# Column slices of 256, 424 and 424 in place of 336, 384 and 384, and one feature tile pair for all columns

## The chip, the cores and the metric

The kernel runs on one core of one Trainium2 chip. The metric is the device time of one execution in microseconds (us). The profile is one execution taken by the hardware profiler; its engines are called PE (TensorE), PEld (TensorE's weight loads), DVE (VectorE), ACT (ScalarE), POOL (GpSimd) and SP (SyncE, which here only issues transfers).

## The reference, cut to what matters

One inference step of a two-layer decoder: an mLSTM layer and a forgetting-attention (FoX) layer, each with an output projection added to the hidden state and a SwiGLU FFN behind it. There are 1104 token columns: 64 sample tokens and 16 meta tokens (together 80), then 1024 prompt tokens. The width D is 1024, the FFN's 2816, all float32.

```python
xn = rmsnorm(x, g)
p  = xn @ w_in                        # q, k, v, output gate, gates i and f
h, state = mlstm_sequence(q, k, v, li, lf, state0, lead)
x  = x + (rmsnorm(h, mh_g) * sigmoid(og)) @ w_out
a, b = split(rmsnorm(x, g_f) @ w_gate_up)
x  = x + (silu(a) * b) @ w_down       # FFN, once in each layer
...
x  = x + (o * sigmoid(og)) @ w_out    # second layer; o: attention with per-row log-forget values
...
x  = x + (silu(a) * b) @ w_down
y  = rmsnorm(x, g_final)
```

## The kernel before, in words

**Layout.** Activations lie feature-major: 128 features on the partitions, 8 such blocks (KT) for D, and tokens as columns. The columns are cut into three slices TS; each is made of three token tiles (the first tile has 80 tokens, the others 128): 336, 384 and 384 columns, SL = 384. A matmul loads a 128x128 block of weights and moves one slice of columns through it.

**Precision.** Every float32 operand is split into a high and a low fp32r part (L243 on ACT, L244 on DVE), and a product is three matmuls: high by high, high by low, low by high (L170 to L172).

**The features of the current layer step** stand in `X[t]`, a pair of tiles (high, low) for each slice, allocated anew by `new_x` whenever the features are written again, which orders the new writer behind the readers of the old tile. Reading a token tile goes through `x_tile`.

**Layer 0.** `phase_a` loads and norms the tokens, projects them, and runs the mLSTM over chunks. The values of all heads stand in three tiles `vA`. `gate_head` (L1247) transposes a head's result (PE L1256), multiplies it with the output gate read back from HBM by POOL (DVE L1257, in tiles ogqk, ogeb, ogc), and splits it into the features.

**The output projection** (`mlp`, L395) has a `unit(t, m)` for each slice t and output block m: 24 matmuls, an addition into the hidden state (DVE L462) and its squares for the norm. In layer 0 the units of slice 0 run between the gating of the later heads, and the weights of m = 0 to 2 (`wo`) come split from HBM by six SP loads (L440), that of m = 3 (`woraw`) is loaded raw and split, and m = 4 to 7 come raw through two slots and are split there (L447). In layer 1 all eight come raw through two slots. Stores of the mLSTM's end state (`out_p_C`, `out_p_n`, L967 and L968) are also issued by SP; out_p_n is written in elements of four bytes.

**The FFN** (`ffn`, L1263) computes slice 0 plainly and slices 1 and 2 together by Winograd's form of Strassen's product: seven products in place of eight, of halves of the weights, slices and features. The up projection has 22 `Unit`s a layer: 48 plain matmuls of slice 0 (two column blocks of w_gate and w_up, 24 each, tile fps) and 84 product matmuls (L1314). The down projection (L1633, tile dps) has 528 plain and 924 product matmuls a layer. The operands of the products are sums and differences of slices, made by DVE; at the FFN's start `TwoNorms` (L90 to L151) norms slice 2 and makes these for the first time, while PE runs the plain blocks of the first Units. Results of the up projection go to HBM (hT, hB) and come back through POOL's queue (`hr`, L1454).

**The end of layer 0's FFN** feeds `first_values` (L1725), which reads token tiles of the normalized features; `final` (L1674) norms, transposes (tile fin) and stores the output of a slice in three token tiles, two halves of the width each (DVE L1715), with the sums of squares from PE (tile fss, L1698).

**What sets the order.** PE's order is the program's, by hand, in the projections and the FFN; in the FFN's start and loop DVE's and ACT's are as well. The queues of SP and POOL, and DVE and ACT in layer 0's output projection, are ordered by a list scheduler, so that a change of sizes can move instructions there.

Of the kernel before, what the change touches and what calls it, by code (L numbers as in the profile page):

```python
# [16 lines left out]
P = 128  # L17
D = 1024
KT = D // P
# [10 lines left out]
TS = [(TT[g[0]][0], TT[g[-1]][1]) for g in GRP]  # L30
SL = max(b - a for a, b in TS)
# [14 lines left out]
class PairWeights:  # L46

    def __init__(self, net, w, slots, H):  # L50
        self.net, self.w = net, w
        cut = lambda t, a=0: t[:, a : a + KT * P].rearrange("p (k n) -> p k n", k=KT)
        flat = [h.rearrange("p k n -> p (k n)") for h in H]
        self.raw = [(cut(slots[0]), cut(slots[1])), (cut(flat[0]), cut(flat[0], KT * P)),
                    (cut(flat[2], 4 * SL), cut(flat[1], 2 * KT * P))]
        self.both = [(cut(slots[2 + i]), cut(slots[6 + i])) for i in range(4)]
# [33 lines left out]
class TwoNorms:  # L90
# [63 lines left out]
class Net:  # L154
# [109 lines left out]
    def new_x(self, t):  # L264

        n = TS[t][1] - TS[t][0]
        self.X[t] = tuple(
            self.xp.tile([P, KT, n], F32R, name=self.uid(f"x{t}{s}"), tag=f"x{t}{s}") for s in "hl"
        )
        return self.X[t]  # L270

    def x_tile(self, i, k):

        t = i // 3
        o = TS[t][0]
        a, b = TT[i][0] - o, TT[i][1] - o
        xh, xl = self.X[t]
        return xh[:, k, a:b], xl[:, k, a:b]
# [44 lines left out]
    def norm_x(self, H, t, g, sp, pp, inplace=False, psum=False):  # L323
# [8 lines left out]
        for i in GRP[t]:  # L332
            yield
            rs = r[:, TT[i][0] - t0 : TT[i][1] - t0]
            nc.vector.reciprocal(rs, rs)
        xh, xl = self.new_x(t)
# [38 lines left out]
    def run(self):  # L375
        nc, tc, I, O, ctx = self.nc, self.tc, self.I, self.O, self.ctx
        self.consts()
        self.hD = self.dram.tile([P, KT, T], F32, name="hD")
        self.X = {}
        self.wmin = 0  # L380
        self.slots = None
        cy, cb = ExitStack(), ExitStack()
        with ExitStack() as c1:
            self.xp = c1.enter_context(self.pool("x"))
            with ExitStack() as c2:

                vp = c2.enter_context(self.pool("vH"))
                vt = [vp.tile([P, 3 * HA * (DV + 1)], F32, name=f"vA{t}") for t in range(3)]
                heads = self.phase_a(vt)
                H = [v[:, : KT * (t1 - t0)].rearrange("p (k n) -> p k n", k=KT) for v, (t0, t1) in zip(vt, TS)]  # L390
# [162 lines left out]
def load_x(self):  # L553

    nc, I = self.nc, self.I
    with self.pool("lx", bufs=2) as lp, self.pool("lxp", bufs=2, space=PSUM) as pp:
        gr = lp.tile([P, D], F32, name="gr", bufs=1)
        nc.scalar.dma_start(gr, I["norm_a"][0].partition_broadcast(P))
        for i, (t0, t1) in enumerate(TT):
            n = t1 - t0  # L560
            if i % 3 == 0:
                self.new_x(i // 3)
# [14 lines left out]
            for g in range(2):  # L577
# [5 lines left out]
                o = t0 - TS[i // 3][0]  # L583
                xh, xl = self.X[i // 3]
                self.split(ps[:, :, :n], xh[:, ks, o : o + n], xl[:, ks, o : o + n])
# [9 lines left out]
def phase_a(self, vt):  # L595
# [4 lines left out]
    v = lambda i: vt[i // 3][:, i % 3 * HA * (DV + 1) : (i % 3 + 1) * HA * (DV + 1)].rearrange(  # L600
        "p (h d) -> p h d", h=HA)
    with ExitStack() as c3:
# [88 lines left out]
        def heads(pp, tag, op=None, some=None):  # L691
# [4 lines left out]
            def ahead():  # L696
                if todo:
                    t, h = todo.pop(0)
                    og = op(self.uid("ogc")) if callable(op) else op.pop(0)
                    nc.gpsimd.dma_start(og[:, : TS[t][1] - TS[t][0]], ogD[h, :, TS[t][0] : TS[t][1]])  # L700
                    ready.append(og)
# [174 lines left out]
def recurrence(self, kp, rec, v, qkD, fill, gate):  # L876
# [12 lines left out]
    with ExitStack() as cr, self.pool("recAp", bufs=2, space=PSUM) as pp:  # L889
# [28 lines left out]
        with self.pool("rec2") as sets[2], self.pool("rec1", bufs=2) as rp, self.pool("rec3") as sets[0]:  # L918
# [8 lines left out]
            for i in range(1, NT):  # L927
# [16 lines left out]
                if i in (6, 7):  # L944

                    for x in ("qk", "eb"):
                        y = sets[i % 3].tile([P, 1024], F32, name=f"og{x}{i}", tag=x,
                                             bufs=2 if x == "eb" and i == 7 else None)
                        places += [y[:, z : z + SL] for z in (0, 512)]
# [297 lines left out]
def gate_head(self, t, h, v, og, pp, tag):  # L1247

    nc = self.nc
    yh, yl = self.X[t] if h else self.new_x(t)  # L1250
    g0, g1 = TS[t]
# [7 lines left out]
    self.split(og[:, :n], yh[:, h, :], yl[:, h, :])  # L1259
# [3 lines left out]
def ffn(self, H, l, weights, order, norm, each, after, end, early=None):  # L1263
# [16 lines left out]
    with self.pool(f"ffn{l}") as fp, self.pool(f"ffnp{l}", space=PSUM) as pp:  # L1280
# [4 lines left out]
        fs += [flat[0][:, 2048 : 2048 + SL]] + [flat[2][:, a : a + SL] for a in (0, SL, 2 * SL, 3 * SL, 2560)]  # L1285
# [170 lines left out]
        def h_split(y):  # L1456
            if y < len(hseq):
# [3 lines left out]
                else:  # L1461
                    o = [y for t, n in ((0, 3), (1, 4), (2, 4)) for y in cut(self.X[t], n)][c]
                r = hraw.pop(y)
                m, n = r.shape[1:]
                hpart[t, z if t else 0, c] = tuple(p[:, : m * n].rearrange("p (k n) -> p k n", k=m) for p in o)
# [208 lines left out]
def final(self, H, t, gr, sp, pools):  # L1674
# [3 lines left out]
    s0 = TS[t][0]  # L1678
    r = sp.tile([P, 3], F32, name=self.uid("fr"), tag="fr", bufs=2)
# [4 lines left out]
    out = [out[:, x % 5 * 512 : x % 5 * 512 + 512] for x in range(6)]  # L1684

    def turn(i, t0, t1):
# [8 lines left out]
    def root():  # L1695
        ss = pn.tile([P, 512], F32, name=self.uid("fss"), tag="n")
        for y, (_, a, b) in enumerate(tiles):
# [9 lines left out]
    for x, (i, t0, t1) in enumerate(tiles):  # L1707
        L = t1 - t0
        ps = turn(i, t0, t1)
        if t == 2 and x == 0:  # L1710
            root()
        for g in range(2):
# [4 lines left out]
            if i == 0:  # L1717
                nc.sync.dma_start(O["y_sample"].rearrange("b t d -> (b t) d")[:, gs], o[:NS])
            else:
                nc.sync.dma_start(O["y_prompt"][0, (i - 1) * P : i * P, gs], o)  # L1720
# [4 lines left out]
def first_values(self, fp, pp, norm):  # L1725
# [4 lines left out]
    for t in range(3):  # L1730
        vs = self.ny(f"vf{t}").rearrange("p k t -> p (k t)").rearrange("p (i d) -> p i d", i=3)
# [59 lines left out]
def phase_b(self, ys, w7, cb):  # L1791
# [11 lines left out]
    with self.pool("fb", bufs=2) as fp, self.pool("fbp", bufs=2, space=PSUM) as pp:  # L1803
# [38 lines left out]
        for w, g, gi, dst, dstS in ((wkv, G_KV, 0, self.kD, self.kS), (wqo, G_B, 1, self.qD, self.qS)):  # L1842
            gcol = gc[:, gi : gi + 1]
            for c in range(4):
# [12 lines left out]
                def turn(q, v4, c=c, raw=raw, gi=gi, gcol=gcol, dst=dst, dstS=dstS):  # L1857
                    for hp in range(2):
                        f = 2 * c + hp
                        ps = pp.tile([P, 512], F32, name=self.uid("btp"), tag="bt")  # L1860
                        g0, g1 = TS[q]
# [5 lines left out]
                        hi = fp.tile([P, SL], F32R, name=self.uid("bhi"), tag="bhi")  # L1867
                        lo = fp.tile([P, SL], F32R, name=self.uid("blo"), tag="blo")
# [71 lines left out]
def forget(self, lf):  # L1940

    nc, I, O = self.nc, self.I, self.O
    with self.pool("fg") as fp, self.pool("fgp", bufs=1, space=PSUM) as pp:
# [9 lines left out]
        for q in range(3):  # L1953
            ps = pp.tile([HB, 512], F32, name=f"fgps{q}", tag="fg")
            g0, g1 = TS[q]
# [311 lines left out]
def attend_prompt(self, ys):  # L2267
# [3 lines left out]
    with self.pool("ap", bufs=1) as sp, self.pool("ap2", bufs=2) as s2, self.pool("app", bufs=2, space=PSUM) as pp:  # L2271
# [159 lines left out]
        def units(hp, g):  # L2431
# [8 lines left out]
            for j0 in range(0, nf, 2):  # L2440
# [32 lines left out]
                def prod(j0=j0, tail=tail, hold=hold):  # L2473
# [54 lines left out]
        with tc.manual_schedule(engines={E.PE, E.DVE, E.Activation, E.Pool}):  # L2528
# [22 lines left out]
            for hp, g in groups:  # L2551
                us = None
                for k in range(g + 1):
                    n = len(todo_exp)
                    ahead(slot)
                    if slot == 0:
                        for _ in gate:
                            pass
                        for t in range(3):
                            self.new_x(t)  # L2560
# [53 lines left out]
```

## Time and profile before

| | |
|---|---|
| time, median of 3 runs | 2905.01 us (2904.12 to 2905.68) |
| span of the profiled execution | 2904.6 us |
| PE busy | 97% |
| DVE, ACT, POOL busy | 58%, 40%, 28% |
| mean granted PE clock | 0.991 |
| HBM traffic | 159 GB/s over the span |

A row of a group or of the timeline gives the line of the kernel, the engine, the tile written and those read, their shapes and the time; in the chain of waits each row is the start, the length and the piece of work that led to the end. "x84" is a count of instructions. In a table of stretches the columns are the stretch, its length, the busy time of PE, PEld, DVE, ACT and POOL (with the number of instructions), the granted PE clock, the share of the DMA engines, and GB/s. Matmul durations overlap, since matmuls are pipelined; some of their records are missing.

### The profile page before, as it was taken

To read this page: it belongs to the slowest core of one execution; us is meant where nothing else is said; L and a number is where in the kernel's file an instruction comes from. 1 tells how busy PE (TensorE), PEld (TensorE's weight loads), DVE (VectorE), ACT (ScalarE), POOL (GpSimd) and SP (SyncE) were. 2 spreads that over 40 slices of the span, in tenths; PEclk is the share of its full clock that TensorE was granted. 3 is DMA by queue.
4 is the path that set the end of the run, shared out by engine and by line. 5 is a ranking of instruction groups with operands and counts; after the bars stand their busy time and mean duration, and the time that the engine had idled before them with its cause. 6 is when DMAs were issued, how large, how long until landed. Compare 5 with 4: busy or idle time off the path is not lost.

```text
span 2904.6 us, 53405 instructions
## 1 busy us (share of the span) xinstructions
PE 2819.4 (97%) x20709; PEld 2702.2 (93%) x20709; DVE 1687.8 (58%) x3292; ACT 1151.6 (40%) x2103; POOL 827.6 (28%) x1225
## 2 busy tenths in 40 slices
PE   7999989999999999999999899999999999999998
PEld 7999879999999999999999787677899999999998
DVE  5032565876776555672445443777477677655565
ACT  5222463422222244453444444877332222224343
POOL 2021232332232221134352101454323223222122
PEclk9999999999999999999999999999999999999999
DMA  7153555244444375664454775443324444437574
GB/s 249 49 142 96 138 172 148 89 148 148 148 150 152 107 259 198 225 210 130 137 169 130 235 280 201 131 163 105 121 95 149 147 148 151 152 106 237 185 248 145
DMA packets 381625, 464.43 MB, mean 160 GB/s; under 512 B 37571, under 2 KB 302747, under 8 KB 380347
## 3 DMA queue, kind: packets, MB, share of 16 engines
q1 hardware_dynamic: 341058, 323.68, 35.1%
q0 software_dynamic: 37904, 135.88, 14.5%
q8 instruction: 163, 2.67, 0.4%
q10 hardware_dynamic: 2408, 1.46, 0.2%
q14 instruction: 92, 0.75, 0.1%
HBM read 324.63 MB, written 136.29 MB: 159 GB/s over the span
## 4 chain that ended last, share of the span: by engine, by line
PE 78%; DVE 6%; ACT 2%; issue 2%; DMA 2%; POOL 0%; DVEq 0%; SPq 0%; ACTq 0%; POOLq 0%
PE m L1314 21%; PE dps L1633 16%; PE fps L172 4%; PE fps L171 4%; PE fps L170 4%; PE tmps L170 3%; PE tmps L171 3%; PE tmps L172 3%; PE sp L2401 2%; PE pops L172 1%; PE pops L170 1%; PE pops L171 1%; PE op L2488 1%; DVE s L2405 1%; PE mmA L170 1%
## 5 line engine op out<-in xcount | busy, mean ns | idle before, releaser
L244 DVE TENSOR_TENSOR slot<-slot,slot 128x1024 fp32r<-128x1024 f32 (+1 forms) x152 | 194.8, 1283 | 141.5 <-ACT slot L243 141.1
L243 ACT CAST slot<-slot 128x1024 fp32r<-128x1024 f32 (+1 forms) x152 | 152.9, 1007 | 200.1 <-PE dps L1633 98.7
L172 PE MATMUL fps<-x0h,slot 128*128 128x336 f32 x688 | 218.2, 317 | 1.6 <-DVE slot L244 1.6
L170 PE MATMUL fps<-x0h,slot 128*128 128x336 f32 x688 | 218.0, 317 | 0.0
L171 PE MATMUL fps<-x0l,slot 128*128 128x336 f32 x688 | 217.4, 316 | 0.0
L1314 PE MATMUL m<-x2h,slot 128*128 128x384 f32 x704 | 193.7, 336 | 0.0
L1314 PE MATMUL m<-x1h,slot 128*128 128x384 f32 x672 | 185.0, 336 | 0.0
L172 PEld LDWEIGHTS fps<-x0h,slot 128*128 128x128 f32 x688 | 129.1, 188 | 2.1 <-DVE slot L244 2.1
L170 PEld LDWEIGHTS fps<-x0h,slot 128*128 128x128 f32 x688 | 129.3, 188 | 0.6 <-ACT slot L243 0.5
L171 PEld LDWEIGHTS fps<-x0l,slot 128*128 128x128 f32 x688 | 129.5, 188 | 0.1
L1314 PEld LDWEIGHTS m<-x2h,slot 128*128 128x128 f32 x704 | 128.5, 188 | 0.0
L1314 PEld LDWEIGHTS m<-x1h,slot 128*128 128x128 f32 x672 | 122.5, 188 | 0.1
L1633 PE MATMUL dps<-T_1h,slot 128*128 128x384 f32 x448 | 118.9, 340 | 0.0
L1314 PE MATMUL m<-x2l,slot 128*128 128x384 f32 x352 | 118.4, 336 | 0.0
L1633 PE MATMUL dps<-T_2h,slot 128*128 128x384 f32 x448 | 117.6, 338 | 0.0
L244 DVE TENSOR_TENSOR slot<-Ht,slot 128x1024 fp32r<-128x1024 f32 x59 | 83.7, 1418 | 54.5 <-ACT slot L243 54.5
L244 DVE TENSOR_TENSOR slot<-vA,slot 128x1024 fp32r<-128x1024 f32 x59 | 83.7, 1418 | 54.5 <-ACT slot L243 54.5
L1314 PE MATMUL m<-x1l,slot 128*128 128x384 f32 x336 | 112.8, 336 | 0.0
L321 POOL TENSOR_TENSOR ns<-ns,nq 128x384 f32<-128x384 f32 (+1 forms) x62 | 75.5, 1218 | 106.0 <-ACT nq L319 104.1
L1314 PE MATMUL m<-T_2h,slot 128*128 128x384 f32 x352 | 97.8, 338 | 2.0 <-DVE slot L244 2.0
L2428 ACT ACTIVATE s<-s,nb 128x272 f32<-128x272 f32 (+7 forms) x126 | 98.9, 787 | 0.0
L1314 PE MATMUL m<-T_4h,slot 128*128 128x384 f32 x352 | 97.8, 338 | 0.6 <-DVE vA L1295 0.6
(783 smaller groups left out, 9157.1 us busy)
## 6 DMA issues: line engine op xcount, KB each, us to landing
slot<-in_w_down SPq DMA_DIRECT2D x48, 512.0 KB, 4.6
slot<-in_w_gate_up SPq DMA_DIRECT2D x36, 512.0 KB, 4.2
ws<-in_w_down SPq DMA_DIRECT2D x88, 192.0 KB, 2.9
sD<-ws SPq DMA_DIRECT2D x88, 192.0 KB, 2.1
kp<-in_cache_k SPq DMA_DIRECT2D x32, 512.0 KB, 6.1
vp<-in_cache_v SPq DMA_DIRECT2D x32, 512.0 KB, 5.5
hr<-hB_T POOLq DMA_DIRECT2D x40, 384.0 KB, 5.1
vA<-in_w_gate_up SPq DMA_DIRECT2D x26, 512.0 KB, 3.9
```

The source lines that it names most:

```text
L170: mm(ps, sh, mh, start=first, stop=False)
L171: mm(ps, sh, ml, start=False, stop=False)
L172: mm(ps, sl, mh, start=False, stop=last)
L243: self.nc.scalar.copy(hi, src)
L244: self.nc.vector.tensor_tensor(out=lo, in0=src, in1=hi.bitcast(F32), op=ALU.subtract)
L321: (nc.vector if x >= late else nc.gpsimd).tensor_tensor(out=s, in0=s, in1=sq, op=ALU.add)
L1314: nc.tensor.matmul(u.ps[b], w[p][:, k], x[q][:, k], start=first and k == i == 0, stop=k == 3 and i == 2, skip_group_check=True)
L1633: nc.tensor.matmul(o, p[:, k, ms], q[:, k], start=fresh and k == x == 0, stop=last and k == nk - 1 and x == 2, skip_group_check=True)
L2401: nc.tensor.matmul(ps[z][:, :n], a[r, qs], b[r, at : at + n], start=(y == 0), stop=(y == 2))
L2405: nc.vector.tensor_tensor_reduce(out=ss[z, u][:, at + o : at + e], in0=ps[z][:, o:e], in1=diag[x][:, z] if y else ncb[:, z, at + o : at + ...
L2428: nc.scalar.activation(ss[z, u], ss[z, u], AF.Exp, bias=nb[:, z : z + 1], accum_out=sm[:, u, z : z + 1])
L2488: mm(po[ds[z], :256], vr[:, j0 + x, ds[z]], th[:, x, z], start=(j0 + x == 0), stop=False)
```

## The change

The slices become 256, 424 and 424 columns. They no longer end where token tiles end; where the program goes by token tiles (gating, the attention's transposes, the forget gates) it takes the old groups, now TG with the width GL. The features are one pair of tiles for all 1104 columns, and `X[t]` are views into it; `new_x` is gone. `vA` is one tile. The reciprocals of a norm go in three equal pieces of a slice. One scratch piece of the FFN comes from another pool, as a block that held it is now too small. `final` cuts the slices into pieces of their own: (80, 88, 88), and four of 106 for each of the other two. In the attention, POOL's copies of 256 columns are no longer split at a slice's border. The scratch for descriptors of POOL's DMAs is set to 8192 bytes in the program's constructor, which had no such setting.

```diff
-TS = [(TT[g[0]][0], TT[g[-1]][1]) for g in GRP]
-SL = max(b - a for a, b in TS)
+TG = [(TT[g[0]][0], TT[g[-1]][1]) for g in GRP]
+GL = max(b - a for a, b in TG)
+SL = 424
+TS = [(0, T - 2 * SL), (T - 2 * SL, T - SL), (T - SL, T)]
+def pieces_of(n, m=3):
+    w = -(-n // m)
+    return [(a, min(a + w, n)) for a in range(0, n, w)]
...
     def inverse(self):
-        for x in range(3):
-            self.net.nc.vector.reciprocal(self.r[:, x * P : x * P + P], self.r[:, x * P : x * P + P])
+        for a, b in pieces_of(SL):
+            self.net.nc.vector.reciprocal(self.r[:, a:b], self.r[:, a:b])
...
-        self.x = net.new_x(2)
+        self.x = net.X[2]
...
-    def new_x(self, t):
-        n = TS[t][1] - TS[t][0]
-        self.X[t] = tuple(
-            self.xp.tile([P, KT, n], F32R, name=self.uid(f"x{t}{s}"), tag=f"x{t}{s}") for s in "hl"
-        )
-        return self.X[t]
...
-        t = i // 3
-        o = TS[t][0]
-        a, b = TT[i][0] - o, TT[i][1] - o
-        xh, xl = self.X[t]
-        return xh[:, k, a:b], xl[:, k, a:b]
+        a, b = TT[i]
+        return tuple(x[:, k, a:b] for x in self.xs)
...
+            self.xs = [xp.tile([P, KT, T], F32R, name=f"x{s}") for s in "hl"]
+            self.X = [tuple(x[:, :, a:b] for x in self.xs) for a, b in TS]
...
-                vt = [vp.tile([P, 3 * HA * (DV + 1)], F32, name=f"vA{t}") for t in range(3)]
+                vt = vp.tile([P, NT * HA * (DV + 1)], F32, name="vA")
...
-    yh, yl = self.X[t] if h else self.new_x(t)
-    g0, g1 = TS[t]
+    yh, yl = self.xs
+    g0, g1 = TG[t]
...
-        fs += [flat[0][:, 2048 : 2048 + SL]] + [flat[2][:, a : a + SL] for a in (0, SL, 2 * SL, 3 * SL, 2560)]
+        fs += [self.nq(f"fs{l}q")] + [flat[2][:, a : a + SL] for a in (0, SL, 2 * SL, 3 * SL, 4 * SL + KT * P)]
...
-    tiles = [(i, TT[i][0], TT[i][1]) for i in GRP[t]]
+    a = 0 if t else T0
+    tiles = [(0, T0)] * (t == 0) + [(s0 + a + b, s0 + a + c) for b, c in pieces_of(s1 - s0 - a, 4 if t else 2)]
...
-                    for t, (t0, t1) in enumerate(TS):
-                        a, b = max(c0, t0), min(c0 + 256, t1)
-                        if a < b:
-                            xh, xl = self.X[t]
-                            xs = slice(a - t0, b - t0)
-                            ya = y[:, a - c0 : b - c0]
-                            nc.gpsimd.tensor_copy(xh[:, hp, xs], ya)
-                            nc.gpsimd.tensor_tensor(out=xl[:, hp, xs], in0=ya, in1=xh[:, hp, xs].bitcast(F32),
-                                                    op=ALU.subtract)
+                    xh, xl = (x[:, hp, c0 : c0 + 256] for x in self.xs)
+                    nc.gpsimd.tensor_copy(xh, y)
+                    nc.gpsimd.tensor_tensor(out=xl, in0=y, in1=xh.bitcast(F32), op=ALU.subtract)
...
-    nc = _bacc.Bacc("TRN2", target_bir_lowering=False, num_devices=1)
+    nc = _bacc.Bacc("TRN2", target_bir_lowering=False, num_devices=1, dynamic_dma_scratch_size=8192)
```

More of the change, by code (lines that the diff above doesn't have):

```diff
@@ L331, in norm_x @@
         nc.scalar.activation(r, ps[:, :n], AF.Sqrt, scale=1.0 / D, bias=self.eps)
-        for i in GRP[t]:
+        for a, b in pieces_of(n):
             yield
-            rs = r[:, TT[i][0] - t0 : TT[i][1] - t0]
-            nc.vector.reciprocal(rs, rs)
-        xh, xl = self.new_x(t)
+            nc.vector.reciprocal(r[:, a:b], r[:, a:b])
+        xh, xl = self.X[t]
         if psum:
@@ L378, in run @@
         self.hD = self.dram.tile([P, KT, T], F32, name="hD")
-        self.X = {}
         self.wmin = 0
@@ L1258, in gate_head @@
                                    in1=og[:, :n], op0=ALU.mult, op1=ALU.mult)
-    self.split(og[:, :n], yh[:, h, :], yl[:, h, :])
+    self.split(og[:, :n], yh[:, h, g0:g1], yl[:, h, g0:g1])
 @_add(Net)
@@ L1677, in final, with turn @@
     pp, pn = pools
-    s0 = TS[t][0]
-    r = sp.tile([P, 3], F32, name=self.uid("fr"), tag="fr", bufs=2)
+    s0, s1 = TS[t]
+    r = sp.tile([P, 4], F32, name=self.uid("fr"), tag="fr", bufs=2)
     nc.vector.memset(r, 1.0)
-    tiles = [(i, TT[i][0], TT[i][1]) for i in GRP[t]]
+    a = 0 if t else T0
+    tiles = [(0, T0)] * (t == 0) + [(s0 + a + b, s0 + a + c) for b, c in pieces_of(s1 - s0 - a, 4 if t else 2)]
     out = H[(2, 0, 1)[t]].rearrange("p k n -> p (k n)")
-    out = [out[:, x % 5 * 512 : x % 5 * 512 + 512] for x in range(6)]
-    def turn(i, t0, t1):
+    m = out.shape[1] // 512
+    out = [out[:, x % m * 512 : x % m * 512 + 512] for x in range(2 * len(tiles))]
+    def turn(t0, t1):
         ps = []
@@ L1696, in root @@
         ss = pn.tile([P, 512], F32, name=self.uid("fss"), tag="n")
-        for y, (_, a, b) in enumerate(tiles):
+        for y, (a, b) in enumerate(tiles):
             nc.tensor.matmul(ss[: b - a, y : y + 1], self.sums[t][:, a - s0 : b - s0], self.ones[:, 0:1],
@@ L1706, in final @@
         yield
-    for x, (i, t0, t1) in enumerate(tiles):
+    for x, (t0, t1) in enumerate(tiles):
         L = t1 - t0
-        ps = turn(i, t0, t1)
+        ps = turn(t0, t1)
         if t == 2 and x == 0:
```

41 lines of the change are left out of this document (18 added, 23 removed).

## The prediction

> **What bounds the kernel now.** I read the page first: the span, the engines' shares, and the shares of the chain of waits that ended last.
>
> ```profile
> span 2904.6 us, 53405 instructions
> ...
> PE 2819.4 (97%) x20709; PEld 2702.2 (93%) x20709; DVE 1687.8 (58%) x3292; ACT 1151.6 (40%) x2103; POOL 827.6 (28%) x1225
> ...
> PE 78%; DVE 6%; ACT 2%; issue 2%; DMA 2%; POOL 0%; DVEq 0%; SPq 0%; ACTq 0%; POOLq 0%
> ```
>
> TensorE is the bound, so the change is first a change in matmul time; the part of the chain that is not PE shows where it isn't. Then the chain inside the first FFN's loop (start, duration, what):
>
> ```profile
> 605.51 14.66 PE m L1314 x84
> ...
> 627.58 14.66 PE m L1314 x84
> ```
>
> and the timeline of single matmuls. Their durations overlap, so the distance of starts is what one costs.
>
> ```profile
> 708.30 0.31 PE L170 MATMUL fps<-x0h,slot 128*128 128x336 f32 x1
> ...
> 715.71 0.34 PE L1314 MATMUL m<-x1h,slot 128*128 128x384 f32 x1
> ...
> 1293.77 0.28 PE L171 MATMUL tmps<-slot,x0h 128*128 128x256 f32 x1
> ...
> 1299.91 0.28 PE L172 MATMUL tmps<-slot,x1l 128*128 128x256 f32 x1
> ```
>
> A Unit takes 627.58 − 605.51 = 22.07 us: 84 product matmuls of 384 columns, 14.66/84 = 0.1745 us each, and 48 plain ones of 336 columns (708.30 to 715.71), 7.41/48 = 0.1544 each. Of 256 columns, 53 start between the two tmps rows: 6.14/52 = 0.1181. None with full depth has 424 columns: its price is extrapolated, by the slope from 336 to 384 (0.00042 a column: 0.1912) or in proportion (0.1745 × 424/384: 0.1927).
>
> **The change part by part.**
>
> *Units, 22 in each layer.* 48 × (0.1544 − 0.1181) = 1.74 us saved, 84 × (0.0167 to 0.0182) = 1.40 to 1.53 added: −0.21 to −0.34, taken as −0.28. VectorE doesn't take over the loop (columns: stretch, length, busy time of PE, PEld, DVE, ACT, POOL):
>
> ```profile
> 600.00:1000.00 400.00, 400.00 (x2395) 400.00 (x2394) 273.98 (x379) 107.42 (x145) 119.20 (x78) 1.00 0.45 140
> ```
>
> 274 of 400 us busy; even 10.4% more (424/384) would be 303. The first two Units of each layer belong to the norm stage below, so 40 count: **−11.2** (−8.4 to −13.6). The Trainium skill, "TensorE: Matmul & The Clock Gate" (Wait — 56ns, not 53.3ns?), gives N/2.4 GHz + 2.5 ns between warm matmuls; by it a Unit would gain 48 × 0.0333 − 84 × 0.0167 = 0.20 us, an estimate, and the term would be −8. The rows lie above its values (0.1181 against 0.109), so here the measurement decides.
>
> *Down projections.* By the loops, 528 plain and 924 product matmuls a layer: −19.2 + (15.4 to 16.8), about −3.0 twice: **−6.0** (−4.8 to −7.5).
>
> *Norm of slice 2 at the start of each FFN (TwoNorms, L90-151).* Here VectorE is the bound:
>
> ```profile
> 570.00:580.00 10.00, 9.38 (x54) 8.99 (x53) 9.86 (x13) 2.20 (x3) 0.00 (x0) 1.00 0.41 118
> 580.00:590.00 10.00, 8.23 (x47) 7.32 (x46) 7.80 (x14) 4.63 (x6) 4.85 (x4) 1.00 0.91 272
> ...
> 554.00:588.00 34.00, 15.52 (x12) 1.00 0.47 138
> ...
> 554.00:588.00 34.00, 4.32 (x8) 1.00 0.47 138
> ...
> 554.00:588.00 34.00, 2.58 (x3) 1.00 0.47 138
> ```
>
> The last three are VectorE's busy time in 554 to 588 on L99, L119 and L113 alone: 22.4 us, and all of it grows with the slice; with three more L1295 evacuations in front of the last splits I count 25.5 × 0.104 = +2.7 a layer. TensorE is idle 0.6 + 1.8 us there already, so its shorter plain blocks only lengthen that idle time. **+5.4** for both layers (+3 if half is covered, +6.5 with the square sums ahead of it).
>
> *Output projection of layer 0.* The order of the SP queue moves. Before:
>
> ```profile
> 413.26 2.91 SPq L440 DMA_DIRECT2D wo<-woD  x6
> ...
> 431.10 0.61 SPq L967 DMA_DIRECT2D out_p_C<-C  x1
> 431.76 0.82 SPq L968 DMA_DIRECT2D out_p_n<-C  x1
> ...
> 438.89 16.38 SPq L447 DMA_DIRECT2D slot<-in_w_out_a  x4
> ...
> DMA to landing us min/median/max: 12.4/12.4/12.4
> ```
>
> In the changed program the four state stores (L967, L968) stand ahead of the six wo loads and of woraw (L447). They wait for VectorE's state update (L1099), so wo, issued at 413.26 before, can issue only after 431, some 15 to 20 us later. The last row is out_p_n from issue to landing. What that store does to the other transfers (last column: GB/s; then the chain; then the projection's first unit and its first slot unit):
>
> ```profile
> 413.00:429.00 16.00, 12.03 (x124) 9.56 (x122) 9.14 (x21) 7.62 (x26) 5.33 (x9) 1.00 0.93 317
> 437.00:439.00 2.00, 2.00 (x15) 2.00 (x14) 1.69 (x5) 1.48 (x8) 1.35 (x3) 0.95 1.12 23
> ...
> 439.46 11.94 DMA slot<-in_w_out_a
> ...
> PE ghps L1256 <- DVE ogc L1257: 5.1, 3, 2.8
> ...
> 436.66 0.63 PE L170 MATMUL pops<-x0h,wo 128*128 128x336 f32 x1
> ...
> 469.24 0.63 PE L170 MATMUL pops<-x0h,slot 128*128 128x336 f32 x1
> ```
>
> While it runs, 23 GB/s move in place of 317, and the 512 KB issued behind it took 11.94 us. The Trainium skill, "DMA: Bandwidth & Descriptors" (Queues, rings and completion order), says that on each DMA engine the descriptors of one issuing engine are consumed in ring order; the 11.94 agrees, and by that rule this order speaks against the change. From the rows: out_p_n has landed at 431.76 + 12.4 = 444.2, or 2 to 3 us sooner, since the gate loads that the state update waits for no longer share with wo; the first pair of wo, 1 MB at 317 GB/s, takes 3.3. So the first unit, at 436.66 before, starts at 442 to 447. From there to the first slot unit (469.24) TensorE waited 5.1 us for L1257, which stands behind weight splits on VectorE, and four plain units in that stretch get 24 × 0.0363 = 0.87 shorter each. But the split of woraw is now queued among those L1257, and they wait for its load. I take +6 at the first slot unit, near the upper half since that load is the last of seven; the ends are −2 (the old waits absorb the delay and half of the 3.5 is kept) and +11 (the delay in full). After it four plain units save 3.5 and fourteen of 424 columns add 24 × 0.0174 = 0.42 each: +2.4. **+8.4** (0 to +13).
>
> *Output projection of layer 1.* Weights come through two raw slots; SP's issues, then the chain:
>
> ```profile
> 2048.48 1.59 SPq L447 DMA_DIRECT2D slot<-in_w_out_b  x2
> ...
> 2056.88 1.50 SPq L447 DMA_DIRECT2D slot<-in_w_out_b  x2
> ...
> 2064.29 2.49 SPq L447 DMA_DIRECT2D slot<-in_w_out_b  x2
> ...
> 2070.15 1.06 ACT wo L243
> ...
> 2072.51 0.42 PE pops L172
> ```
>
> A pair comes every 8 us. Two plain units took 48 × 0.1544 = 7.4 and now take 5.7, so TensorE outruns the supply: the seventh unit still starts at 2072.5, and only the last two units' 1.7 of the 7.0 us saved is kept, while 16 units of 424 columns add 6.4 to 7.0. **+5.0** (0 if the supply follows, +6.5).
>
> *The ends.* The last slice leaves in four pieces instead of three.
>
> ```profile
> 2889.70 1.61 DVE Ht L1295 x4
> ...
> 2897.27 2.90 DVE Ht L1715 x5
> ```
>
> Two more L1715 at 2.90/5 = 0.58 and one more root step add 1.5; the eight more transposes of slice 1 stand on TensorE before, 1.1: **+2.6** (+1 to +3.5). The tile of first_values that straddles the border now needs slice 2's norm, 24 × 0.1181 = 2.8 us sooner: **+0.5** (0 to +1). At the start 32 gathers move ahead of most w_in loads on SP:
>
> ```profile
> 91.77 17.50 SPq L739 DMA_DIRECT2D lp<-in_cache_logf  x32
> ...
> PE tmps L170 <- ACT vA L624: 1.3, 1, 1.3
> ```
>
> The one wait of TensorE in that stretch stands behind weight splits that now come later: **−1.3** (−2.8 to +1.5, where a load that issues up to 17.5 us later is not all hidden by the work between it and its use).
>
> *At nothing:* 16 fewer POOL copies in attention (POOL is busy 28%), views instead of new tiles for the normalized input (TensorE's order stays), and the halved descriptor scratch of POOL's DMAs:
>
> ```profile
> hr<-hB_T POOLq DMA_DIRECT2D x40, 384.0 KB, 5.1
> ```
>
> Those loads are issued ahead of their splits; if the scratch filled, they would be late: 40 × 5.1 = 204 us of landing, of which a twentieth on the path would be 10 (0 to +10).
>
> Sum on the profiled execution: −11.2 − 6.0 + 5.4 + 8.4 + 5.0 + 2.6 + 0.5 − 1.3 = +3.4, span 2904.6 to 2908.0. The median of the runs, 2905.01, is 0.4 above that span: **2908.4**.
>
> **The rivals.**
>
> *Columns alone decide* (faster). The moved loads and the thin supply are hidden by waits that stand there now. Both projections then cost −7.0 + 6.7: −11.2 − 6.0 − 0.6 + 5.4 + 1.8 = −10.6, 2894. For it: 5.1 us of waits ahead of 469. Against: the 11.94 row.
>
> *The stores ahead of the weights decide* (slower). Place: SP's queue from 431 to 445. Price: 13 instead of 8.4, and as TensorE then idles through what the plain units save, the other two stalls at their upper ends: −17.2 + 13 + 6.5 + 6.5 + 1.8 = +10.6, 2916. It decides once the first unit starts after 447.
>
> *The scratch fills* (slower): +10 on the forecast, 2918. Against: nothing but the idle time these loads have.
>
> *The narrow matmul does not get cheaper.* That the change doesn't do what it says: at full depth a floor holds. Were 256 columns to cost what 272 do,
>
> ```profile
> 1314.52 0.28 PE L170 MATMUL tmps<-slot,x0h 128*80 128x272 f32 x1
> ...
> 1317.51 0.29 PE L170 MATMUL tmps<-slot,x0h 128*128 128x272 f32 x1
> ```
>
> 2.99/24 = 0.1246, the 3168 plain matmuls of Units and down projections lose 0.0065 each: +20, 2929. Against: the tmps rows of 256.
>
> **How the numbers follow.** Forecast 0.47, columns alone 0.26, stores ahead 0.17, scratch 0.06, floor 0.04. The forecast's own range is 2900 to 2916. What a measurement can tell from no change is about 0.2%, 5.8 us, so "same" is 2899.2 to 2910.8: the forecast gives 0.30 to it, 0.15 to slower, 0.02 to faster. Faster: 0.26 + 0.02 = 0.28; slower: 0.15 + 0.17 + 0.06 + 0.04 = 0.42. The range of 8 in 10 takes in columns alone and the stores with some of the unknown prices around them: 2891 to 2922.
>
> **What would show it.** The Unit's period at 21.73 to 21.87; the first unit of layer 0's projection after 441 and its first slot unit at 472 to 478; TwoNorms' VectorE stretch 2.7 longer; the seventh unit of layer 1 as far from the first load as before; seven L1715 in the last chain. A period above 22.0, or a first unit still at 437, makes the prediction wrong.

## The result and the profile after

| | before | after |
|---|---|---|
| time, median of 4 runs each | 2904.57 us (2902.58 to 2905.68) | 2987.96 us (2984.84 to 2990.01) |
| span of the profiled execution | 2904.6 us | 2988.3 us |
| mean granted PE clock | 0.991 | 0.980 |

The ratio is 1.0288 (95% interval 1.0274 to 1.0303): 83 us slower, far outside the predicted range of 2891 to 2922. The page of the changed kernel (span; TensorE's share; shares of the chain that ended last):

```profile
span 2988.3 us, 53415 instructions
...
PE 2832.9 (95%) x20729; PEld 2669.0 (89%) x20729; DVE 1708.4 (57%) x3296; ACT 1154.8 (39%) x2105; POOL 821.0 (27%) x1209
...
PE 32%; DVE 4%; DMA 2%; issue 2%; ACT 2%; POOL 0%; SPq 0%; DVEq 0%; ACTq 0%; POOLq 0%
```

TensorE is busy 2832.9 us against 2819.4, 13.5 us more. Some of this may be the lower clock around idle stretches; how much was not worked out. The other 70 us are idle time of TensorE. To find where, I cut the span at first or last starts of matmuls of named tiles, in each profile alike. "start" ends with the first mmA (layer 0's projection), "to pops" with the first unit of the output projection, "pops" is that projection, "up" and "down" are the FFN, "values" runs to the last tmps (layer 1's projections), "to sp" and "attention" to the first score and to layer 1's first pops, "tail" is what follows the last dps.

| us | start | to pops | pops | up | down | values | to sp | attention | pops | up | down | tail | span |
|---|---|---|---|---|---|---|---|---|---|---|---|---|---|
| before | 140.2 | 296.5 | 110.9 | 491.6 | 247.7 | 322.9 | 177.7 | 258.7 | 101.4 | 488.8 | 254.5 | 13.7 | 2904.6 |
| after | 146.9 | 302.2 | 110.1 | 489.8 | 245.5 | 327.8 | 193.0 | 256.3 | 110.3 | 489.0 | 271.3 | 46.1 | 2988.3 |
| difference | +6.7 | +5.7 | −0.8 | −1.8 | −2.2 | +4.9 | +15.3 | −2.4 | +8.9 | +0.2 | +16.8 | +32.4 | +83.7 |

The last two stages, where `final` stores the output, hold +49. The chain of waits of the changed kernel there (start, length, what):

```profile
2900.33 16.71 DMA out_y_prompt<-Ht
...
2923.52 12.96 DMA slot<-sD
...
2951.06 10.43 DMA out_y_prompt<-Ht
```

Before, no store stood in this chain; now 27 us of it are VectorE waiting for a store to free a buffer Ht, and 13 are a weight load behind such stores. And when VectorE's last piece is done, at 2962.4, the stores alone run on to 2988.3, 26 us; before, 3 us followed VectorE's last piece. The stretches show what these stores are (columns as in the prediction; the last two are the share of the DMA engines and GB/s). After:

```profile
2951.00:2961.00 10.00, 3.02 (x16) 2.73 (x14) 3.42 (x6) 0.00 (x0) 0.00 (x0) 0.67 0.13 43
2961.00:2985.00 24.00, 0.00 (x0) 0.00 (x0) 0.75 (x1) 0.00 (x0) 0.00 (x0) 0.50 0.13 51
```

and before, at the same work:

```profile
2898.00:2903.50 5.50, 2.18 (x11) 1.77 (x9) 3.31 (x6) 0.00 (x0) 0.00 (x0) 0.50 0.75 288
```

A share of 0.13 over 24 us in which almost nothing but stores runs is 2 of 16 engines (0.125). They move 51 GB/s, 25 each; before, a share of 0.75, which is as much as 12 engines busy all the time, moved 288, 24 each. So a busy engine is as quick as before, and fewer take part. What changed is the rows of a store: 106 in place of 128. The Trainium skill, "DMA: Bandwidth & Descriptors" (Why a DMA increments its semaphore by 16 and not by 1), says that a transfer goes on the largest number of engines, up to 16, that divides its slowest dimension: 2 for 106 = 2 × 53, 11 for 88, 16 for 128; the trace agrees, with 0.13. The store also holds the issuing queue. SP's timeline, after:

```profile
2899.67 3.90 SPq L1718 DMA_DIRECT2D out_y_prompt<-Ht  x2
...
2908.81 14.30 SPq L1718 DMA_DIRECT2D out_y_prompt<-Ht  x4
2923.52 3.94 SPq L1471 DMA_DIRECT2D slot<-sD  x1
2950.40 23.68 SPq L1718 DMA_DIRECT2D out_y_prompt<-Ht  x8
```

and before:

```profile
2898.05 3.62 SPq L1720 DMA_DIRECT2D out_y_prompt<-Ht  x6
```

A row's time goes from the first issue of its group to the end of the last. Before, the six issues took 0.33 us each and came at the pace of VectorE's pieces, one in 0.66. Now the four from 2908.81 on stand close to each other and fill 14.30 us, since an issue behind stores that are still running takes up to 4.5 us. So the weight load at 2923.52 could not leave before 2923.1.

### The profile page after: what moved, and what is told of

It is laid out like the page before. It is cut to its first block, busy times and chain, and to the rows that moved or that the text cites. A ratio compares the mean times of both kernels' runs of the same rounds, so it can differ in the third digit from the quotient of the medians.

```text
span 2988.3 us, 53415 instructions
## 1 busy us (share of the span) xinstructions
PE 2832.9 (95%) x20729; PEld 2669.0 (89%) x20729; DVE 1708.4 (57%) x3296; ACT 1154.8 (39%) x2105; POOL 821.0 (27%) x1209
## 5 line engine op out<-in xcount | busy, mean ns | idle before, releaser
L1309 PE MATMUL m<-xh,slot 128*128 128x424 f32 x1376 | 399.1, 355 | 0.0
L1309 PEld LDWEIGHTS m<-xh,slot 128*128 128x128 f32 x1376 | 258.7, 188 | 7.3 <-issue 0.2
L1309 PE MATMUL m<-xl,slot 128*128 128x424 f32 x688 | 244.4, 355 | 0.6 <-DVE xl L109 0.6
L180 PE MATMUL tmps<-slot,xh 128*128 128x256 f32 (+2 forms) x864 | 244.7, 283 | 0.0
L181 PE MATMUL tmps<-slot,xh 128*128 128x256 f32 (+2 forms) x864 | 243.4, 282 | 0.0
L182 PE MATMUL tmps<-slot,xl 128*128 128x256 f32 (+2 forms) x864 | 242.9, 281 | 0.0
L182 PE MATMUL fps<-xh,slot 128*128 128x256 f32 x688 | 193.6, 281 | 1.6 <-DVE slot L254 1.6
L181 PE MATMUL fps<-xl,slot 128*128 128x256 f32 x688 | 193.5, 281 | 0.0
L180 PE MATMUL fps<-xh,slot 128*128 128x256 f32 x688 | 193.5, 281 | 0.0
L182 PEld LDWEIGHTS tmps<-slot,xl 128*128 128x128 f32 (+1 forms) x864 | 159.1, 184 | 0.0
L180 PEld LDWEIGHTS tmps<-slot,xh 128*128 128x128 f32 (+1 forms) x864 | 158.5, 183 | 0.2 <-issue 0.2
L181 PEld LDWEIGHTS tmps<-slot,xh 128*128 128x128 f32 (+1 forms) x864 | 158.5, 183 | 0.2 <-issue 0.2
L182 PEld LDWEIGHTS fps<-xh,slot 128*128 128x128 f32 x688 | 130.0, 189 | 2.0 <-DVE slot L254 2.0
L180 PEld LDWEIGHTS fps<-xh,slot 128*128 128x128 f32 x688 | 129.8, 189 | 0.7 <-ACT slot L253 0.4
L181 PEld LDWEIGHTS fps<-xl,slot 128*128 128x128 f32 x688 | 129.6, 188 | 0.3 <-issue 0.2
L181 PE MATMUL mmA<-xl,whi 128*128 128x424 f32 (+1 forms) x384 | 126.4, 329 | 0.0
```

Of the source, the lines that this page charges most:

```text
L180: mm(ps, sh, mh, start=first, stop=False)
L181: mm(ps, sh, ml, start=False, stop=False)
L182: mm(ps, sl, mh, start=False, stop=last)
L1309: nc.tensor.matmul(u.ps[b], w[p][:, k], x[q][:, k], start=first and k == i == 0, stop=k == 3 and i == 2, skip_group_check=True)
```

## The experiments

In each diff "-" and "+" are against the kernel named. Ratios are to the kernel before, run beside it; "stage" is a column of the table above.

**Stores by rows.** e1 is the changed kernel with `final`'s pieces of 112, 96, 96 and 120 rows (96 and 80 in slice 0), as many pieces as in the changed kernel. 112, 96 and 80 are multiples of 16; 120 has 15 as its largest divisor up to 16. e4 is the kernel before with each prompt store cut at row 106, into one of 106 rows and one of 22.

```diff
-    tiles = [(0, T0)] * (t == 0) + [... pieces_of(s1 - s0 - a, 4 if t else 2)]
+    cuts = [s0 + a]
+    for n in ((112, 96, 96, 120) if t else (96, 80)):
+        cuts.append(cuts[-1] + n)
+    tiles = [(0, T0)] * (t == 0) + list(zip(cuts, cuts[1:]))
```

> The changed kernel with other pieces in final: 96 and 80 columns behind the first 80 of slice 0, and 112, 96, 96, 120 in slices 1 and 2, still four pieces. Theory (a y_prompt store of 106 rows moves 51 GB/s, two of 16 DMA engines' share of 0.13, and holds both the end and the weight loads queued behind it on SP): 40 to 50 us faster than the changed kernel, 2938 to 2948; from the last matmul to the end about 15 us instead of 46, the last down projection about 254 instead of 271. Rival (the end is long because four pieces are four times evacuation, transposes and root): as slow as the changed kernel, 2980 to 2990.

```diff
-                nc.sync.dma_start(O["y_prompt"][0, (i - 1) * P : i * P, gs], o)
+                for a, z in ((0, 106), (106, P)):
+                    nc.sync.dma_start(O["y_prompt"][0, (i - 1) * P + a : (i - 1) * P + z, gs], o[a:z])
```

> The kernel before with each 128-row store of y_prompt cut into one of 106 rows and one of 22. Theory: the 106 rows go at about 51 GB/s, 4.2 us each, the last six in a row some 25 us, and the stores of slice 1 hold up weight loads: 2930 to 2955. Rival (width of a store does not matter, only its bytes): 2905 to 2912.

e1 took 2952.02 us, ratio 1.0168 (1.015 to 1.0186): 35 us of the 83 are gone, a little less than the 40 to 50 expected, as the fourth piece keeps a price of its own (see below). Its tail is 16.6 in place of 46.1, its last down projection 260.1 in place of 271.3. SP's timeline of e1, where the weight load now leaves at 2909.61 and eight issues take 4.94:

```profile
2909.61 0.36 SPq L1471 DMA_DIRECT2D slot<-sD  x1
2940.25 4.94 SPq L1721 DMA_DIRECT2D out_y_prompt<-Ht  x8
```

e4 took 2944.06, ratio 1.0145 (1.0122 to 1.0168), with the old columns: tail 37.7 and last down projection 271.2, together 40.7 above those of before. Its SP timeline, and below it a stretch:

```profile
2910.06 20.99 SPq L1721 DMA_DIRECT2D out_y_prompt<-Ht  x12
```

```profile
2923.00:2935.00 12.00, 0.00 (x0) 0.00 (x0) 0.00 (x0) 0.00 (x0) 0.00 (x0) 0.50 0.17 59
```

Taking the row count away costs 35 us less, and putting it in costs 40 more: the two agree that it costs 35 to 40 us. e4 also doubles the number of stores, so its 40 may hold a little more than the row count.

**Which part of the rest is the columns.** e2 is the changed kernel with slices of 384 (pieces of `final`: four of 96, two of 128 in slice 0); e9 is e1's program with slices of 384 and the old three pieces of 128. Both keep the single feature pair, the single vA and the halved scratch.

```diff
-SL = 424
+SL = 384
```

> The changed program with SL = 384, so the old slices of 336, 384, 384, all else as changed (one feature tile pair, one vA tile, four pieces of 96 columns in final, the small scratch). Theory (some 34 us of the loss outside the stores come with the new tiles and the order that they give the queues): 2925 to 2945. Rival (they come with the columns): 2900 to 2912.

```diff
-SL = 424
+SL = 384
...
-    for n in ((112, 96, 96, 120) if t else (96, 80)):
+    for n in ((128, 128, 128) if t else (128, 128)):
```

> The changed program with the old slices (336, 384, 384) and the old pieces of final, 128 columns each. Theory (four pieces instead of three cost the last down projection 5 us and the tail 2): 2911 to 2915, against 2919.6 of e2_old_slices. Rival (the pieces cost nothing where they are stored on all engines): as e2_old_slices, 2917 to 2922.

e2 took 2919.55, ratio 1.0054 (1.0037 to 1.0072); e9 took 2910.9, ratio 1.0033 (1.0021 to 1.0045). By medians, each against the kernel before run beside it, the four steps add up to the change: 8.0 (e9: no new columns, no fourth piece), 7.9 (fourth piece: e2 less e9), 32.5 (columns: e1 less e2), 35.1 (rows: the change less e1). The fourth piece is seen in the last down projection (259.3 in e2, 254.4 in e9) and the tail (15.9 and 13.3), although e2 cuts it into multiples of 16. The runs of e9 lie between 2905.9 and 2919.1 and its profile at 2905.8, so its own 8.0 is the least certain of the four.

By stages, e1 less e2 is: to pops +6.3, to sp +13.9, attention +7.2, layer 1's pops +9.0; first pops −2.9, up −2.8 and −0.8, the others within 1. So the FFN gains 4 us, and what costs lies elsewhere. e2 came between what the theory expected (2925 to 2945: the new tiles) and what the rival did (2900 to 2912: the columns); both have a part. The step called columns also holds all that wider slices do to the places of tiles, which comes next.

**The scratch and the places of tiles.** e3 is the kernel before with the halved descriptor scratch and nothing else.

```diff
-    nc = _bacc.Bacc("TRN2", target_bir_lowering=False, num_devices=1)
+    nc = _bacc.Bacc("TRN2", target_bir_lowering=False, num_devices=1, dynamic_dma_scratch_size=8192)
```

> The kernel before with the descriptor scratch of POOL's DMAs set to 8192 bytes, nothing else. Theory: no change, 2900 to 2910. Rival (a ring of half the size stalls POOL's issue): 2915 to 2940, with POOL's loads of hr landing later than 5.1 us.

2901.96, ratio 0.9997 (0.9987 to 1.0006): nothing, the start 3.1 longer and the attention 7.0 shorter. But the addresses that the programs give their tiles show that the scratch moves nearly all tiles down by 8192 bytes, while the weight slots and some other weight tiles stay, and that wider slices make tiles larger and push others along. In the changed kernel the last wo tile reaches 1216 bytes into the tile eb of the mLSTM (64 bytes clear before), and the third buffer of the layer-1 gate, ogb, which is one slice wide, 192 bytes into qh (288 clear before). Both come from the wider slices: in e3 the same 64 and 288 bytes are clear as before. A tile placed over another has to wait until that one is done with. e11 is e3 with two gaps that bring about just these two overlaps, with old columns and old tiles:

```diff
+                if cb:
+                    wp.tile([P, 320], F32, name="gapA")
...
+        fp.tile([P, 120], F32, name="gapB", bufs=1)
```

> e3_scratch (the kernel before with the small scratch, old slices, old tiles) with two gaps that make the overlaps of the changed kernel and nothing else: 1280 bytes ahead of the wo tiles, so that the last shares 1216 bytes with eb, and 480 bytes ahead of ogb, so that its third buffer shares 192 bytes with qh. Theory (these shared bytes, not the columns, delay the wo and q, k loads): mmA to the first unit 301 to 303 us instead of 295, values to the first score 190 to 193 instead of 179, in all 2918 to 2924 against 2902. Rival (the delays come with slices of 424): 2900 to 2905.

2919.78, ratio 1.0054 (1.0037 to 1.007), 16 us above e3 when each median is set against the kernel before run beside it. To pops is 303.6 (e3: 294.8; first pops then 5.9 shorter), to sp 186.3 (178.7; 190 to 193 were expected), attention 255.8 (251.7). So the wo overlap costs about 3 net, and the qh overlap about 12. SP's timeline of e3:

```profile
413.89 3.23 SPq L440 DMA_DIRECT2D wo<-woD  x6
...
432.37 0.61 SPq L967 DMA_DIRECT2D out_p_C<-C  x1
...
1775.42 0.33 SPq L2221 DMA_DIRECT2D vmS<-vD  x1
1775.79 0.42 SPq L2320 DMA_DIRECT2D qh<-qDh  x1
```

of e11:

```profile
431.74 0.61 SPq L969 DMA_DIRECT2D out_p_C<-C  x1
...
434.77 11.76 SPq L442 DMA_DIRECT2D wo<-woD  x6
...
1777.80 0.33 SPq L2225 DMA_DIRECT2D vmS<-vD  x1
1796.86 0.34 SPq L2324 DMA_DIRECT2D qh<-qDh  x1
```

and of the changed kernel:

```profile
434.30 0.61 SPq L962 DMA_DIRECT2D out_p_C<-C  x1
...
437.11 10.96 SPq L439 DMA_DIRECT2D wo<-woD  x6
...
1790.64 0.33 SPq L2219 DMA_DIRECT2D vmS<-vD  x1
1810.26 0.34 SPq L2318 DMA_DIRECT2D qh<-qDh  x1
```

With 192 and 1216 shared bytes, e11 has the order of the changed kernel in both places: the state stores ahead of wo, and 19 to 20 us between vmS and qh. In the changed kernel's chain of waits one sees what qh waits for, the store of the gate out of ogb:

```profile
1804.08 0.58 POOL og2D L1926
1804.65 3.12 issue
1807.80 2.19 DMA og2D<-ogb
1810.26 0.34 SPq L2318
...
1812.07 9.07 DMA ncb<-cD
```

**Taking the overlaps out of the changed kernel.** e5 is e1 with gaps of 320 and 64 columns that part the tiles; e6 is e5 with the state stores issued by ScalarE, out of SP's queue.

```diff
+        r0.tile([P, 320], F32, name="gapA")
...
+        sp.tile([P, 64], F32, name="gapB")
```

> e1_rows16 with two unused gaps in SBUF: 256 bytes ahead of the attention's tiles, so that qh no longer shares its first 192 bytes with the third gate tile ogb, and 1280 bytes ahead of the mLSTM's tile eb, which the last wo tile overlaps by 1216. SP's order at the state stores stays (stores ahead of wo). Theory (qh waits for the store of the last gate out of those 192 bytes, and SP's queue waits with it): from the last projection of values to the first score 178 instead of 192 us, in all 2936 to 2942. Rival (the longer way there comes from slices of 424): 2948 or more.

```diff
-        nc.sync.dma_start(O["p_C"][0, 0, a::2].rearrange("j k v -> k j v"), cs[:, :, :DV])
-        nc.sync.dma_start(O["p_n"][0, 0, a::2].rearrange("j k -> k j").unsqueeze(2), cs[:, :, DV:])
+        nc.scalar.dma_start(O["p_C"][0, 0, a::2].rearrange("j k v -> k j v"), cs[:, :, :DV])
+        nc.scalar.dma_start(O["p_n"][0, 0, a::2].rearrange("j k -> k j").unsqueeze(2), cs[:, :, DV:])
```

> e5_gaps with the four state stores issued by ACT instead of SP, so that four of the six wo loads issue ahead of them and the last two and woraw behind them. Theory (wo behind the stores costs some 7 us at the first unit of layer 0's projection): from the first mmA to that unit 297 to 299 instead of 303 us, in all 4 to 6 us less than e5_gaps. Rival (old waits hide it): as e5_gaps.

e5: 2944.68, ratio 1.015 (1.0133 to 1.0167). To sp went from e1's 191.9 to 183.4, where 178 was expected; the queue now stops at ql, three loads behind qh. SP's timeline of e5:

```profile
1788.42 0.37 SPq L2323 DMA_DIRECT2D kl<-kDl  x1
1803.12 0.32 SPq L2323 DMA_DIRECT2D ql<-qDl  x1
```

SP waited 14.3 us there for TensorE's gate product (bps, L181). The addresses tell why: the gap of 64 columns pushes ql 192 bytes into a weight slot that this product reads (64 bytes clear in e1). The gap took one overlap out and made another, which e6, e7 and e10 keep.

To pops stayed at 301.6: the stores still stand ahead of wo although those tiles no longer overlap. So in the changed kernel the wo overlap is not all that sets this order, and what else does is open. e6: 2939.77, ratio 1.0121 (1.0102 to 1.0141). To pops fell to 295.2, 6.4 less, but the projection behind it became 2.7 longer: these stores ahead of the weights cost 3.7 net.

**The gathers at the start.** In the changed kernel the 32 gathers lp are issued ahead of most w_in loads; lp lay over a raw weight tile before and no longer does. This comes from the scratch: e3 has it too. e7 is e6 with a gap ahead of lp, e12 is e3 with the running sums' tiles first and a gap, both to put lp back over that tile.

```diff
+        sp.tile([P, 2274], F32, name="gapC")
```

> e6_state_on_act with a third gap of 9096 bytes ahead of lp, so that it shares bytes with a raw weight tile again and the 32 gathers stand behind the weight loads on SP, as in the kernel before. Theory (the weight loads behind the gathers cost the start some 5 us): first mmA at 141 instead of 146 us, in all 4 to 6 us less than e6_state_on_act. Rival (the start is longer by the matmuls that read the one tile pair): as e6_state_on_act, first mmA at 145 or later.

```diff
+        cs = sp.tile([P, PAST], F32, name="cs")
+        lt = sp.tile([P, PAST], F32, name="csl")
+        on = sp.tile([P, PAST], F32, name="cso")
+        sp.tile([P, 738], F32, name="gapC")
...
-        cs = sp.tile([P, PAST], F32, name="cs")
-        lt = sp.tile([P, PAST], F32, name="csl")
-        on = sp.tile([P, PAST], F32, name="cso")
```

> e3_scratch with the tiles of the cache's preparation in another order and a gap ahead of lp, so that lp shares bytes with a raw weight tile as before and the gathers issue behind the weight loads. Theory (the early gathers cost the start 3 us, the smaller scratch frees the attention's loads): first mmA at 140 instead of 143 us, in all 2896 to 2900, faster than the kernel before. Rival (the shift moves other loads and takes it back): 2901 to 2906.

Both did at the start what was expected, 142.4 against e6's 145.8 and 138.4 against e3's 143.3. Both lost it behind: to pops rose by 16.1 and 9.5. e7 took 2950.97, ratio 1.0161 (1.0144 to 1.0178), slower than e6; e12 took 2903.68, ratio 0.9994 (0.9985 to 1.0003). The waits show a part of it. In e7 ScalarE stood still 9.4 us for csE, a transfer of the running sums that the gathers feed, and TensorE 9.0 us behind it at rps (L818; 0.3 in e6). In e12 ScalarE stood still 10.0 us for VectorE's lse, and TensorE 4.3 behind it at mmA. The gap moved no tiles but lp and those of the running sums; where the rest of the 16.1 and 9.5 went is open.

**Layer 1's output projection.** e10 is e6 with the units of slice 0 and slice 1 mixed, so that the narrow units don't come in one row:

```diff
-                    for m in range(KT):
+                    for m in range(5):
...
+                    for m in range(3):
+                        unit(1, m, m)
+                        unit(0, 5 + m, 5 + m)
...
-                    for m in range(KT):
+                    for m in range(3, KT):
                         unit(1, m, m)
+                        next(run, None)
                         next(run, None)
```

> e6_state_on_act with another order of units in layer 1's output projection: five units of slice 0, then slices 1 and 0 in turn (three each), then the rest of slice 1, so that each new weight has 7.4 us of matmuls instead of 2.8. Theory (slice 0 at 256 columns outruns the weights that come through two raw slots): the projection takes 102 to 106 us instead of 111, in all 5 to 8 us less than e6_state_on_act (2939.8). Rival (its extra time is that of the longer matmuls and of VectorE): 109 to 112 us, in all the same.

2936.33, ratio 1.0101 (1.0086 to 1.0116); the stage fell from 111.3 to 104.1. So about 7 us of this stage were TensorE outrunning its weights. By medians, each against the kernel before run beside it, e10 is 5.8 below e6. The profiled spans differ by 2.7 only, since other stages came out 1 us longer here and there. e13 is e12 with the same order of units, on the old columns:

> e12_gathers_last with the order of units of e10_two_slices in layer 1's output projection. Theory (the old slices outrun the weight supply a little too): the projection 98 to 100 us instead of 101.4, in all 1 to 3 us less than e12_gathers_last. Rival (the supply keeps up at 336 columns): as e12_gathers_last, or slower by the later norm of slice 0.

2903.6, ratio 0.9996 (0.9986 to 1.0005): as e12, and the stage stayed at 101.3. At 336 columns the weights keep up, as the rival said. No version was faster than the kernel before. Columns of 424 with every other cost undone were not tried.

## Why the prediction was wrong, point by point

**The ends: +2.6 predicted, +49 measured. This is the step that failed.** It counted the fourth piece as two more L1715, one root step and eight transposes, the work of VectorE and TensorE, and names no store. What it lacked was the rows of the stores that the pieces end in, on how many engines 106 rows go, and what stands behind them on SP. The row count costs 35 to 40, the fourth piece about 8 more. The sign it named, seven L1715 in the last chain, did not come: there stand two of them (now L1713), 10.43 us of waiting for a store, then one.

**The way to the attention: not in the sum, +15.3.** "At nothing" looked at what a scratch holds and at the order of TensorE, not at where tiles lie. e11 shows the two shared pieces of memory at about 16 us with nothing else changed, in the two places that the changed kernel shows. The one at qh is 7.6 of these up to the first score and 4.1 in the attention; of the +15.3 the other half was not traced. The rival "the scratch fills" did not come: e3 has the same scratch at no cost.

**Layer 0's output projection: the mechanism was right, the size too large.** The changed kernel's timeline of TensorE:

```profile
449.06 0.58 PE L180 MATMUL pops<-xh,wo 128*128 128x256 f32 x1 [8.66 <-DMA wo<-woD]
...
479.39 0.36 PE L180 MATMUL pops<-xh,slot 128*128 128x256 f32 x1
```

As the start is 6.7 later, that is taken off to compare: 442.4 and 472.7, inside the predicted "after 441" and "472 to 478". The first is 5.7 later than before and the first slot unit 3.5, where +6 was taken: two fifths of the delay vanish in the old waits. The two stages together are +4.9, not +8.4. e6 confirms the cause, at 3.7 net. "The stores ahead of the weights decide" needed a first unit after 447 and did not come. "Columns alone decide" needed −0.3 in each projection; they came at +4.9 and +8.9.

**Units: −11.2 predicted, about −4.8.** TensorE's timeline, after:

```profile
703.60 0.35 PE L1309 MATMUL m<-xh,slot 128*128 128x424 f32 x1
...
719.87 0.28 PE L180 MATMUL fps<-xh,slot 128*128 128x256 f32 x1
...
725.55 0.35 PE L1309 MATMUL m<-xh,slot 128*128 128x424 f32 x1
...
747.51 0.35 PE L1309 MATMUL m<-xh,slot 128*128 128x424 f32 x1
```

The 48 plain matmuls take 5.68/48 = 0.1183 each, as priced. The 84 products take 16.27/84 = 0.1937, above both ends of the extrapolation (0.1912 and 0.1927). The period is 21.95 instead of 22.07, 0.12 × 40 = 4.8 us; 21.73 to 21.87 was the sign named. The floor for narrow matmuls did not show. The same price makes a down projection's 924 products 924 × 0.0192 = 17.7 dearer, against 528 × 0.0361 = 19.1 saved: −1.3 a layer in place of −3.0; the first one's stage shows −2.2.

**The norm of slice 2: +5.4 predicted, less came.** VectorE's busy time in the three formulas, after (L109, L129 and L123 are L99, L119 and L113 of before):

```profile
554.00:620.00 66.00, 16.99 (x12) 1.00 0.40 123
...
554.00:620.00 66.00, 4.66 (x8) 1.00 0.40 123
...
554.00:620.00 66.00, 2.83 (x3) 1.00 0.40 123
```

24.48 against 22.42, so 2.1 more where 22.4 × 0.104 = 2.3 was implied for these three. On the path, the up stages of e1 less e2 are −2.8 and −0.8, and 20 Units are −2.4 in each: −0.4 and +1.6 are left for it.

**One feature pair in place of views "at nothing": about +4 in layer 1's projections.** Consecutive L170 matmuls of tmps on slice 1, before:

```profile
1457.89 0.28 PE L170 MATMUL tmps<-slot,x1h 128*128 128x256 f32 x1
...
1465.37 0.28 PE L170 MATMUL tmps<-slot,x1h 128*128 128x256 f32 x1
```

and in e9, which has the single pair and the old columns:

```profile
1463.12 0.28 PE L180 MATMUL tmps<-slot,xh 128*128 128x256 f32 x1
...
1470.93 0.28 PE L180 MATMUL tmps<-slot,xh 128*128 128x256 f32 x1
```

Both stretches hold 22 steps of three matmuls: 7.48/66 = 0.1133 each, and 7.81/66 = 0.1183. Slice 1's are a third of 2592, so 864 × 0.005 = 4.3 us, and the stage is 4.2 longer in e9 than in e3. Why slice 1's own tiles were quicker is open.

**Layer 1's output projection: +5.0 predicted, +8.9.** Reason and sign were right. SP's timeline, after:

```profile
2073.92 1.70 SPq L446 DMA_DIRECT2D slot<-in_w_out_b  x2
...
2081.49 2.04 SPq L446 DMA_DIRECT2D slot<-in_w_out_b  x2
...
2089.43 2.25 SPq L446 DMA_DIRECT2D slot<-in_w_out_b  x2
```

A pair still comes every 7.6 to 7.9 us; the supply does not follow. The measured +8.9 lies above even the upper end of 6.5. Of the narrow units' 7.0 not 1.7 was kept, but 2.3 was lost: from the first matmul of slice 0 to the first of slice 1 it is 2111.92 − 2071.62 = 40.3 us, before 2084.21 − 2046.18 = 38.0. TensorE now waits at the third, fifth and seventh unit for the splits of the weights, up to 2.0 us at once; before, no wait there reached 0.3. The other 6.6 are the 16 wide units, inside the predicted 6.4 to 7.0. So the error is in the narrow units: they lost time where some was to be kept.

**The start: −1.3 predicted, +6.7.** The gathers ahead of the loads cost about 3 to 5 (e12 against e3, e7 against e6; e3 against before is 3.1), so the upper end of +1.5 was too low: the loads were not hidden. The other 2 to 4 were not traced; e2, with the old columns, has them too (146.2).

## What to carry to other kernels

Before a tile size is chosen for TensorE, follow it to the transfers that it cuts: keep the rows of a store a number with 16 among its divisors (112 and 96 did well here, 106 did not), and look at the queue that issues it, since a slow issue delays the loads behind it. After any change of a tile's size or of a reservation, compare the addresses of tiles that belong to neighbouring stages, because a few hundred shared bytes are a wait that no line of the code shows. Compare them again after a gap that is to part two tiles: here one such gap made the next overlap. A matmul width outside those in the trace is better bounded well above the extrapolation: a gain of 1.3% in the loop lost more than half to a price 1% higher.

## What the runs showed of the hardware

- Stores of 106 rows in a row move 51 GB/s with a DMA share of 0.13, the stores of 128 rows 288 GB/s with 0.75. An issue of a 128-row store on SP took 0.33 us; of a 106-row one, behind others that were still running, up to 4.5.
- At full depth a matmul of 424 columns costs 0.1937 us in the products, of 384 columns 0.1745, of 256 columns 0.1183 (and 0.1133 on slice 1's own tiles in layer 1's projections, before): from 384 to 424 it costs 0.00048 a column, from 336 to 384 0.00042.
- Around waits of TensorE the granted clock was lower. Two stretches of the changed kernel, just after idle time at the start and in the wait for qh, stand at 0.83 and 0.76, where the loop of the first FFN stands at 1.00:

```profile
100.00:110.00 10.00, 10.00 (x74) 10.00 (x74) 4.01 (x4) 4.39 (x9) 0.00 (x0) 0.83 0.37 105
1800.00:1820.00 20.00, 10.15 (x52) 8.74 (x52) 1.05 (x5) 4.02 (x6) 1.54 (x4) 0.76 0.45 175
```
